# K's transposes moved from the tensor engine to a transposing DMA, with a retuned instruction order and a new ending, in a grouped-query attention kernel

## The chip, the cores and the metric

The kernel runs on one core of one Trainium2 chip. The metric is the device time of one execution in microseconds (us). Engines are named as in the profile: PE is the tensor engine (PEld its weight loads), ACT the scalar engine, DVE the vector engine, POOL GpSimd, SP the engine that only issues DMAs here. "Span" is the length of one profiled execution; the device time is about 1.8 us more.

## The reference

```python
batch, seq, n_heads, n_kv_heads, dim = 8, 512, 32, 8, 64      # float32 in and out
K_expanded = np.repeat(K, 4, axis=2); V_expanded = np.repeat(V, 4, axis=2)
scores  = np.einsum('bhqd,bhkd->bhqk', Q, K_expanded) / np.sqrt(dim)
weights = np.exp(scores - np.max(scores, axis=-1, keepdims=True))
weights = weights / (np.sum(weights, axis=-1, keepdims=True) + 1e-10)
output  = np.einsum('bhqk,bhkd->bhqd', weights, V_expanded)
```

## The kernel before

Work is cut into 32 units (8 batches, 4 pairs of KV heads). A unit has 16 score tiles of 128 x 1024. For each, PE makes two matmuls into one of three score buffers in PSUM (the pools that hold PE's results); then ACT exponentiates the tile (11 of 16), or DVE approximates the exponential with one multiply-add on the bits (5 of 16; one of these five, the "two-term" tile, gets two more operations on POOL). Between score tiles PE does "filler": blocks of weights times V (4 matmuls each), and transposes of Q and K. Filler goes through two further PSUM buffers, which DVE has to empty.

The order of all this is fixed when the program is built, by a small planner in the kernel that walks through these tables:

```python
TILES  = [int(c) for c in "0100010001020100"]   # per score tile: 0 ACT, 1 DVE, 2 DVE + POOL
SCORES = "ADAAADAADAADAADA"                     # order in which PE makes tiles for ACT and DVE
FILL   = [0, 0, 8, 0, 0, 6, 9, 0, 0, 8, 0, 0, 12, 0, 0, 9]   # filler pieces after each (sum 52)
ORDER  = "K4 o6 o7 08 o7 18 o5 o7".split()      # groups: K4 = K's 4 transposes, o6 = 6 output
SKIP   = 22                                     # blocks, 08/18 = 8 transposes of half of Q
```

SKIP is the number of filler slots left empty at the start, so it sets the phase of the groups against the fills. K arrives and is turned so:

```python
def load_k(b):
    t = kn_pool.tile([128, SC, KV * D], BF16, name="k_nat")
    nc.gpsimd.dma_start(out=t, in_=rows(K, b, 0, KV))
    kn[b] = t
...                                    # mm_turn: 4 PE transposes per unit into a filler buffer
    nc.tensor.transpose(xs[f][:, at * 128:(at + 1) * 128], src, ident)
...                                    # take_turn: one DVE copy, then two DMAs swap the halves
    nc.vector.tensor_copy(out=k[:, 0, :], in_=x[:, 0:S])
    nc.sync.dma_start(out=k[64:128, 1, :], in_=k[0:64, 0, :])
    nc.sync.dma_start(out=k[0:64, 1, :], in_=k[64:128, 0, :])
```

The softmax here doesn't subtract the row's maximum and nothing guards it: scores larger than these inputs give would overflow.

## Time and profile before

| kernel before | |
|---|---|
| device time | 352.62 us median of 4 runs (352.34 to 353.13) |
| span of the profiled run | 351.0 us |
| steady unit, from the starts of every 11th exponential | 10.34 us |
| last exponential starts | 338.8 us, 12.1 us before the end |

The first fence is from the page of the kernel before: busy time and share of the span by engine, then the chain of work that ended last, by engine and by line.

```profile
PE 336.7 (96%) x5774; PEld 224.7 (64%) x5774; DVE 331.3 (94%) x462; ACT 333.1 (95%) x355; POOL 280.2 (80%) x200
...
PE 54%; ACT 37%; DVE 3%; issue 2%; POOL 2%; DMA 1%; POOLq 0%; DVEq 0%; ACTq 0%
```

Three engines are all nearly full, and the chain alternates between two of them. A chain that alternates suggests that neither is the limit alone.

The next lines are groups of instructions of the kernel before (line, engine, operation, out<-in, shape, count | busy us, mean ns | idle before). They are the exponentials, K's transposes and the copies after them; the last two are what the change removes.

```profile
L270 ACT ACTIVATE pa<-s 128x1024 bf16<-128x1024 f32 x352 | 330.6, 1029 | 2.3 <-PE s L259 1.9
...
L382 PE MATMUL x<-ident,k_nat 128*128 128x128 bf16 x124 | 17.3, 222 | 0.0
...
L389 DVE COPY kt<-x 128x512 bf16<-128x512 bf16 x31 | 11.3, 365 | 0.0
```

The mean durations mislead here, because successive instructions overlap. What one costs an engine that is full is the step from its start to the start of the next. In the trace, exponentials follow each other at 0.903 us when nothing holds them up (not 1.029), K's transposes at 0.057 us (not 0.222) and the K copy at 0.278 us (not 0.365). ACT therefore needs 11 x 0.903 = 9.94 us per unit, and a unit takes 10.34.

The timeline of ACT shows the same (start us, length us, what, count, idle before it). One line is an unbroken run; its length over its count is the real pace, 316.10/336 = 0.941 us, which times 11 is 10.35 us.

```profile
7.90 10.19 ACT L270 ACTIVATE pa<-s 128x1024 bf16<-128x1024 f32 x11 [1.00 <-PE s L259]
18.34 316.10 ACT L270 ACTIVATE pa<-s 128x1024 bf16<-128x1024 f32 x336 [0.25 <-PE s L259]
```

Finally the end of the kernel before, from the chain of waits (start us, us, what). The last exponential is over at 339.9 us. The chain waits for POOL's two-term sum until 341.1, then for the last blocks, and then DVE divides until 346.5.

```profile
337.63 1.27 POOL hi L297
...
338.98 2.13 POOL sum L303
...
341.16 1.08 PE x L314 x29
...
343.07 2.22 issue
...
346.05 0.42 DVE o_sb L355
```

The 2.22 us called "issue" lie inside one division of 128 x 512 on DVE, which by DVE's timeline ran from 343.04 us for 2.33 us.

### The profile page before, as it was taken

How to read it: one execution, taken by the hardware profiler on the slowest of the kernel's cores; microseconds unless marked ns; L12 is line 12 of the kernel's file. 1: busy time of each engine (PE TensorE's matmuls, PEld its weight loads, DVE VectorE, ACT ScalarE, POOL GpSimd, SP SyncE). 2: the span in 40 equal slices, each digit the busy share in tenths (PEclk: the TensorE clock that was granted, in tenths of full speed). 3: DMA queues.
4: the chain of work that ended last, by engine and by line, in shares of the span. 5: the costliest groups of instructions: out<-in, count | busy, mean ns of one | idle time of the engine just before them, and what ended most of it. 6: DMA issues, size and time to landing. Idle time of an engine off the chain costs nothing.

```text
span 351.0 us, 12943 instructions
## 1 busy us (share of the span) xinstructions
PE 336.7 (96%) x5774; PEld 224.7 (64%) x5774; DVE 331.3 (94%) x462; ACT 333.1 (95%) x355; POOL 280.2 (80%) x200
## 2 busy tenths in 40 slices
PE   8799999999999999999999999999999999999981
PEld 3366666666666666666666666666666666666661
DVE  3899999999999999999999999999999999999984
ACT  3999999999999999999999999999999999999960
POOL 6368897879978797987979799787988879768783
PEclk9999999999999999999999999999999999999997
DMA  8999567997769968698787985699586997822356
GB/s 184 209 155 185 156 170 194 199 224 168 174 161 240 256 133 209 129 238 202 196 196 167 209 197 160 177 224 251 115 207 153 237 232 183 208 79 78 121 181 181
DMA packets 51479, 64.40 MB, mean 183 GB/s; under 512 B 3424, under 2 KB 36064, under 8 KB 51424
## 3 DMA queue, kind: packets, MB, share of 16 engines
q0 software_dynamic: 25344, 24.91, 47.1%
q1 hardware_dynamic: 25024, 38.28, 32.0%
q8 instruction: 45, 0.74, 0.8%
q10 hardware_dynamic: 1056, 0.39, 0.4%
q14 instruction: 10, 0.08, 0.1%
HBM read 50.86 MB, written 33.55 MB: 241 GB/s over the span
## 4 chain that ended last, share of the span: by engine, by line
PE 54%; ACT 37%; DVE 3%; issue 2%; POOL 2%; DMA 1%; POOLq 0%; DVEq 0%; ACTq 0%
ACT pa L270 37%; PE s L259 24%; PE x L314 22%; PE x L382 7%; DMA kt<-kt 1%; PE x L461 1%; DVE pd L287 1%; POOL sum L303 1%; POOL o_sb L355 1%; DVE raw L334 0%; POOL hi L297 0%; PE x L473 0%; DVE kt L474 0%; DVE inv L350 0%; DVE qt L396 0%
## 5 line engine op out<-in xcount | busy, mean ns | idle before, releaser
L270 ACT ACTIVATE pa<-s 128x1024 bf16<-128x1024 f32 x352 | 330.6, 1029 | 2.3 <-PE s L259 1.9
L259 PE MATMUL s<-qt,kt 64*128 64x512 bf16 x1024 | 163.4, 381 | 3.8 <-DVE pd L287 1.5
L287 DVE TENSOR_SCALAR pd<-s 128x1024 uint16<-128x1024 f32 x128 | 156.0, 1219 | 1.7 <-PE s L259 1.6
L314 PEld LDWEIGHTS <-pa 128*128 128x128 bf16 x2816 | 136.1, 97 | 28.9 <-issue 28.9
L314 PE MATMUL x<-v,pa 128*128 128x65 bf16 x2728 | 150.9, 194 | 0.3 <-DVE raw L334 0.3
L314 PE MATMUL x<-v,pd 128*128 128x65 bf16 x992 | 134.2, 194 | 0.0
L355 POOL TENSOR_TENSOR o_sb<-raw,inv 128x1024 f32<-128x1024 f32 x63 | 118.6, 1907 | 2.9 <-DVE inv L350 2.5
L314 PEld LDWEIGHTS <-pd 128*128 128x128 bf16 x1024 | 100.2, 98 | 0.5 <-issue 0.4
L259 PEld LDWEIGHTS <-kt 64*128 64x128 bf16 x1024 | 56.1, 93 | 68.1 <-issue 37.2
L334 DVE COPY raw<-x 128x455 f32<-128x455 f32 (+3 forms) x161 | 92.8, 578 | 6.6 <-PE x L314 5.8
L297 POOL TENSOR_TENSOR hi<-lo,shift 128x512 int32<-128x512 int32 x32 | 40.6, 1269 | 50.1 <-PE x L314 38.7
L303 POOL TENSOR_TENSOR sum<-lo,hi 128x1024 bf16<-128x1024 bf16 x32 | 68.0, 2125 | 2.5
L382 PE MATMUL x<-ident,q_nat 128*128 128x128 bf16 x504 | 43.8, 220 | 0.0
L396 DVE COPY qt<-x 128x1024 bf16<-128x1024 bf16 x63 | 42.9, 681 | 0.0
L287 DVE TENSOR_SCALAR lo<-s 128x1024 uint16<-128x1024 f32 x32 | 39.2, 1224 | 0.5 <-PE s L259 0.5
L314 PE MATMUL x<-v,sum 128*128 128x65 bf16 x248 | 34.7, 194 | 1.1 <-POOL sum L303 1.1
L382 PEld LDWEIGHTS <-q_nat 128*128 128x128 bf16 x504 | 29.9, 98 | 7.9 <-issue 7.9
L314 PEld LDWEIGHTS <-sum 128*128 128x128 bf16 x256 | 25.0, 98 | 1.2 <-POOL sum L303 1.2
L229 POOL DMA_DIRECT2D q_nat<-in_Q_dram x32 | 25.5, 797 | 0.0
L247 POOL COPY v<-v_nat 128x2048 bf16<-128x2048 bf16 x8 | 15.2, 1904 | 5.7 <-DMA v_nat<-in_V_dram 5.7
L382 PE MATMUL x<-ident,k_nat 128*128 128x128 bf16 x124 | 17.3, 222 | 0.0
L382 PEld LDWEIGHTS <-k_nat 128*128 128x128 bf16 x124 | 7.5, 98 | 7.1 <-issue 7.1
(36 smaller groups left out, 67.6 us busy)
## 6 DMA issues: line engine op xcount, KB each, us to landing
out_dram<-o_sb SPq DMA_DIRECT2D x30, 1024.0 KB, 5.2
q_nat<-in_Q_dram POOLq DMA_DIRECT2D x31, 512.0 KB, 6.0
k_nat<-in_K_dram POOLq DMA_DIRECT2D x8, 512.0 KB, 8.2
v_nat<-in_V_dram POOLq DMA_DIRECT2D x8, 512.0 KB, 10.5
kt<-kt SPq DMA_DIRECT2D x62, 64.0 KB, 5.2
out_dram<-o_sb SPq DMA_DIRECT2D x3, 512.0 KB, 3.0
q<-in_Q_dram ACTq DMA_DIRECT2D x1, 256.0 KB, 4.4
k<-in_K_dram SPq DMA_DIRECT2D x1, 256.0 KB, 3.9
```

The lines of the kernel that those rows point to most:

```text
L229: nc.gpsimd.dma_start(out=t[:, :, lo * D:], in_=rows(Q, b, HU * gp + lo, HU * (gp + 1)))
L247: nc.gpsimd.tensor_copy(out=t[:, :, :, 0:D], in_=vn.pop(b).rearrange("p sc (h d) -> p sc h d", h=KV))
L259: nc.tensor.matmul(s[:, m, :], kt[u][64 * m:64 * m + 64, 0 if m == g else 1, kc * 128:(kc + 1) * 128], qt[u][64 * m:64 * m + 64, i, :], st ...
L270: recent.append(nc.scalar.activation(out=pts[t], in_=score.pop(t), func=mybir.ActivationFunctionType.Exp, scale=float(scale),))
L287: nc.vector.tensor_scalar(out=bits, in0=score.pop(t), scalar1=float(A_schr), scalar2=float(B_two if two else B_one), op0=mybir.AluOpType.mult,
L297: nc.gpsimd.tensor_tensor(out=high.rearrange("p m s -> p (m s)").bitcast(I32), in0=bits.rearrange("p m s -> p (m s)").bitcast(I32), in1=shift,
L303: nc.gpsimd.tensor_tensor(out=dst, in0=bits.bitcast(BF16), in1=high.bitcast(BF16), op=mybir.AluOpType.add)
L314: nc.tensor.matmul(xs[f][:, at * D1:(at + 1) * D1], pts[(u * HPG + i) * SC + kc][:, m, qc * 128:(qc + 1) * 128], v1[u][:, kc, 2 * i // HPG ...
L334: nc.vector.tensor_copy(out=raws[u][:, lo:lo + n, :], in_=x[:, 0:n * D1])
L355: eng.tensor_tensor(out=osbs[u].rearrange("p qc h d -> p h qc d")[:, lo // SC + h0:lo // SC + h0 + nh], in0=src[:, :, 0:D].rearrange("p (h ...
L382: nc.tensor.transpose(xs[f][:, at * 128:(at + 1) * 128], src, ident)
L396: nc.vector.tensor_copy(out=qt[u][:, 2 * part:2 * part + 2, :], in_=x)
```

## The change

The intent: take K off PE and DVE, refit the order to the freed time, and shorten the end.

```diff
-    TILES = [int(c) for c in "0100010001020100"]
-    SCORES = "ADAAADAADAADAADA"
-    FILL = [0, 0, 8, 0, 0, 6, 9, 0, 0, 8, 0, 0, 12, 0, 0, 9]
-    ORDER = "K4 o6 o7 08 o7 18 o5 o7".split()
-    SKIP = 22
+    TILES = [int(c) for c in "0100010201000100"]
+    SCORES = "ADAADAAADAADAADA"
+    FILL = [0, 0, 7, 0, 0, 6, 0, 7, 0, 9, 0, 0, 7, 0, 0, 12]
+    ORDER = "o7 o7 08 o7 o4 18 o7".split()
+    LAST_TILES = [int(c) for c in "0000100111000100"]
+    LAST = {
+        NU - 2: ("AADADADAAADAADAA", [3, 0, 0, 3, 0, 7, 0, 0, 32, 0, 32, 0, 21, 3, 0, 18]),
+        NU - 1: ("DADADAAADAAAADAA", [0, 0, 0, 7, 0, 0, 32, 0, 0, 32, 0, 10, 10, 0, 0, 10]),
+    }
+    SKIP = 15
 # K of batches 1 to 7 (batch 0 stays on PE, units 2 and 3 now also in the start):
+        ks[b] = ks_pool.tile([S, KV * D], BF16, name="ks")          # in DRAM
+        nc.gpsimd.dma_start(out=ks[b], in_=K[b].rearrange("s h d -> s (h d)"))
+    def turn_k(b):
+        straight[b] = kt_pool.tile([128, GP, S], BF16, name="straight")
+        nc.sync.dma_start_transpose(out=straight[b], in_=ks.pop(b))
+    def swap_k(b): ...
+        nc.sync.dma_start(out=k[0:64], in_=t[64:128])
+        nc.sync.dma_start(out=k[64:128], in_=t[0:64])
 # issued one unit apart, a batch ahead:
+                if r == 4 and b + 1 < B:
+                    load_k(b + 1)
+                if r == 20 and b + 1 < B:
+                    turn_k(b + 1)
+                if r == 40 and b + 1 < B:
+                    swap_k(b + 1)
 # the ending: last exponential in two halves; the last output groups first sum over three
 # quarters of the keys ("open"), then add the last quarter ("close"); more divisions from PSUM
+        for ms in (slice(0, 1), slice(1, 2)) if t == 16 * NU - 1 else (slice(0, 2),):
+    groups += [(step, NU - 1, lo, 4) for step in ("open", "close") for lo in (3 * BLK, 3 * BLK + 4)]
 # ... planner support for the above, store and divide split for the last units: cut
```

## The prediction

> **What bounds it now.** Three engines are nearly full: PE 96%, ACT 95%, DVE 94% of 351.0 us (busy table). In the middle the kernel repeats per unit (16 score tiles: 11 exponentials on ACT, 5 on DVE). From the starts of the exponentials in the timeline, a unit takes 10.34 us. Back to back, exponentials start 0.903 us apart, so ACT needs 11 x 0.903 = 9.94 us. Summing the shortest start-to-start steps of the DVE instructions gives 9.95 us per unit. PE's steps without its waits for score buffers come to about 9.7 us (an estimate). So 0.40 us per unit is lost because three score buffers couple three engines without slack; the chain of waits alternates between PE (54%) and ACT (37%).
> The tail is loose: the last exponential starts at 338.8 us, yet the span ends at 351.0. The chain there goes DVE, POOL shift and sum (to 341.1), PE, four DVE divisions (to 346.5), store.
>
> **What changes.** (1) For batches 1 to 7, K is cast into DRAM and transposed by a DMA issued from SP; two larger DMAs swap the halves. This removes 4 PE transposes per unit (0.057 us each from start to start, 0.23 us) and one DVE copy (0.278 us start to start), 28 times. (2) Fill sizes and the place of the two-term tile are retuned. (3) The last unit has no POOL sum, splits its last exponential, sums three quarters of the last outputs before it ends, and moves the divisions.
> ACT keeps its 352 tiles (one split).
>
> **On the critical path.** Per unit, DVE falls to about 9.67 us and PE to 9.47; ACT stays at 9.94 and becomes the only limit. I expect 10.10 us per unit: about 60% of the 0.40 us lost comes back; the score buffers still make a few exponentials wait. 0.24 x 31 = 7.4 us. Tail: after the last exponential about 0.1 us extra for the split, a quarter of the last matmuls, one or two divisions of 0.5 us, then the 4.5 us that ran from the last division to the end before: 7 to 8 us instead of 12.2, so about 4.5 us. The start is unchanged.
> Sum: 352.6 - 7.4 - 4.5 = 340.7 us. I predict **340.7 us**, range **336.5 to 346.0**; faster by over 2%: 0.87; within 2%: 0.12; slower by over 2%: 0.01.
>
> **The transposing DMA.** The trace has none. The Trainium skill ("DMA: Bandwidth & Descriptors", "Latency and other measured facts") gives transposes 261 GB/s; estimated from it, 512 KB take 2 us plus a few us as the other transfers do here (K loads land in 8.2 us). The program leaves one unit (10 us) between cast and transpose, 1.25 between transpose and swap, 1.5 until use. So it should be hidden. The same page ("Anatomy of one DMA") says a semaphore wait sits on the issuing sequencer; if the transpose takes over about 20 us, SP holds up the output stores behind it.
>
> **What would show it.** PE transposes of K fall from 124 to 12, kt copies likewise from 31 to 3. Starts of the exponentials 10.0 to 10.2 us per unit. ACT leads the chain of waits, PE's share falls.  The exponentials end near 331 us and the span ends 7 to 8 us after the last one starts. No wait on the transposed K.
>
> **What would make it wrong.** The retuned order may couple worse than I assume (unit still 10.3: about 347 us) or nearly perfectly (9.96: about 336). The transposing DMA may be much slower, or crowd the Q loads (the DMA share is already 0.81 to 0.89 in the middle), delaying transposes or stores. Larger fills in the last two units may starve ACT and eat the tail's gain.

## The result, and the profile after

The changed kernel takes 345.85 us median (345.1 to 346.2, 8 runs) against 352.71 us (13 runs) for the kernel before: ratio 0.9803, 95% interval 0.9794 to 0.9813. A ratio here is the mean time of one kernel's fast runs over that of the other's of the same rounds, so not quite the ratio of the medians. That is 2.0% faster, exactly at the line between "same" and "faster", so the verdict is "unclear": certainly shorter, but not certainly by 2%. The median lies inside the predicted range by 0.15 us.

The profiled run of the changed kernel was its slowest (348.0 us, span 346.2). So I had the same kernel profiled once more, on the chip of the first batch of experiments (first experiment below): span 344.4 us, time 346.2. Both profiles are used.

From the page of the changed kernel, the same two parts:

```profile
PE 332.6 (96%) x5662; PEld 220.9 (64%) x5662; DVE 317.6 (92%) x435; ACT 330.3 (95%) x356; POOL 274.7 (79%) x199
...
ACT 62%; PE 24%; issue 4%; DVE 4%; POOL 3%; DMA 1%; SPq 0%; DVEq 0%; POOLq 0%
```

The chain now leads through ACT (62%, and 71% in the second profile). The removed groups are gone but for batch 0, as these groups show:

```profile
L423 PE MATMUL x<-ident,k_nat 128*128 128x128 bf16 x12 | 1.5, 223 | 0.0
L430 DVE COPY kt<-x 128x512 bf16<-128x512 bf16 x3 | 1.3, 419 | 0.8 <-PE x L423 0.8
```

The timeline of ACT in the second profile of the changed kernel: the long run has a pace of 300.12/323 = 0.929 us, 10.22 us per unit. But the start is broken into pieces, and so is the end from 320 us on, which in the kernel before was one run until 334.

```profile
7.90 4.74 ACT L306 ACTIVATE pa<-s 128x1024 bf16<-128x1024 f32 x5 [0.94 <-PE s L293]
12.79 1.02 ACT L306 ACTIVATE pa<-s 128x1024 bf16<-128x1024 f32 x1 [0.15 <-PE s L293]
14.17 4.81 ACT L306 ACTIVATE pa<-s 128x1024 bf16<-128x1024 f32 x5 [0.36 <-PE s L293]
19.43 300.12 ACT L306 ACTIVATE pa<-s 128x1024 bf16<-128x1024 f32 x323 [0.45 <-PE s L293]
320.00 2.85 ACT L306 ACTIVATE pa<-s 128x1024 bf16<-128x1024 f32 x3 [0.44 <-PE s L293]
323.55 1.94 ACT L306 ACTIVATE pa<-s 128x1024 bf16<-128x1024 f32 x2 [0.70 <-PE s L293]
```

The end, from the timeline of DVE (second profile). There is no POOL sum and no long division in it; DVE is done 2.6 us after the last tile's first half began (338.53 us), where in the kernel before it took 7.6 us from the last tile's start (338.83 to 346.47).

```profile
338.72 0.42 DVE L396 TENSOR_TENSOR o_sb<-x,inv 128x256 f32<-128x256 f32 x1
339.98 0.18 DVE L391 RECIPROCAL inv<-x 128x4 f32<-128x4 f32 x1 [0.83 <-PE x L352]
340.20 0.42 DVE L396 TENSOR_TENSOR o_sb<-x,inv 128x256 f32<-128x256 f32 x1
340.54 0.17 DVE L391 RECIPROCAL inv<-x 128x4 f32<-128x4 f32 x1
340.75 0.42 DVE L396 TENSOR_TENSOR o_sb<-x,inv 128x256 f32<-128x256 f32 x1
```

Cutting each profiled span at the starts of the exponentials tells where the time went. The two columns in the middle are experiments that follow. All figures are us.

| stretch | before | ending only | middle only | changed (second profile) |
|---|---|---|---|---|
| to the first exponential | 7.90 | 7.38 | 7.90 | 7.90 |
| units 0 to 3 | 41.45 | 41.67 | 41.99 | 42.36 |
| units 4 to 29 (26 units) | 269.02 | 269.00 | 265.53 | 265.52 |
| unit 30 | 10.45 | 13.74 | 10.20 | 12.54 |
| unit 31, to its last tile | 10.01 | 11.21 | 9.73 | 10.21 |
| from there to the end | 12.13 | 5.89 | 12.66 | 5.91 |
| span | 351.0 | 348.9 | 348.0 | 344.4 |

So the middle gives 3.5 us (0.134 us in each of 26 units), the ending gives 6.2 us after the last tile's start but costs 2.3 us in units 30 and 31, and the start costs 0.9 us. The exponentials as a whole are over no earlier than before: the last tile starts at 338.5 against 338.8 us.

In the first profile the start cost more: units 0 to 3 took 44.70 us. PE stood still twice with nothing to wait for that the profile shows, and unit 3 took 12.28 us in place of 10.22. (Another 0.7 us lies in unit 1, where PE waited 0.6 us for POOL's two-term sum.) The experiments come back to the pauses.

### The profile page after: what moved, and what is told of

Same layout as the page of the kernel before. It is cut to its first block, busy times and chain, and to the rows that moved or that the text cites. A ratio compares the mean times of both kernels' runs of the same rounds, so it can differ in the third digit from the quotient of the medians.

```text
span 346.2 us, 12636 instructions
## 1 busy us (share of the span) xinstructions
PE 332.6 (96%) x5662; PEld 220.9 (64%) x5662; DVE 317.6 (92%) x435; ACT 330.3 (95%) x356; POOL 274.7 (79%) x199
## 4 chain that ended last, share of the span: by engine, by line
ACT 62%; PE 24%; issue 4%; DVE 4%; POOL 3%; DMA 1%; SPq 0%; DVEq 0%; POOLq 0%
ACT pa L306 62%; PE x L352 11%; PE s L293 11%; PE x L423 3%; DVE pd L323 2%; DMA v<-in_V_dram 1%; DVE raw L375 1%; POOL sum L339 1%; POOL v L281 1%; POOL q_nat L248 0%; POOL hi L333 0%; DVE inv L391 0%; DVE qt L437 0%; DVE lo L323 0%; DVE o_sb L396 0%
## 5 line engine op out<-in xcount | busy, mean ns | idle before, releaser
L396 POOL TENSOR_TENSOR o_sb<-raw,inv 128x1024 f32<-128x1024 f32 (+1 forms) x64 | 118.5, 1867 | 50.9 <-DVE inv L391 50.9
L293 PE MATMUL s<-qt,straight 64*128 64x512 bf16 x448 | 142.8, 382 | 1.0
L293 PE MATMUL s<-qt,swapped 64*128 64x512 bf16 x448 | 141.8, 381 | 0.3 <-ACT pa L306 0.3
L375 DVE COPY raw<-x 128x455 f32<-128x455 f32 (+1 forms) x159 | 87.9, 570 | 14.2 <-PE x L352 14.2
L339 POOL TENSOR_TENSOR sum<-lo,hi 128x1024 bf16<-128x1024 bf16 x31 | 65.9, 2126 | 2.4
L293 PEld LDWEIGHTS <-straight 64*128 64x128 bf16 x448 | 36.1, 93 | 31.6 <-issue 21.4
L293 PEld LDWEIGHTS <-swapped 64*128 64x128 bf16 x448 | 33.0, 93 | 21.3 <-issue 13.9
L323 DVE TENSOR_SCALAR lo<-s 128x1024 uint16<-128x1024 f32 x31 | 37.7, 1215 | 0.0
L293 PE MATMUL s<-qt,kt 64*128 64x512 bf16 x128 | 21.3, 381 | 2.9 <-ACT pa L306 0.9
```

Source lines behind the costliest of these rows:

```text
L293: nc.tensor.matmul(s[:, m, :], kt[u][int(m != g)][64 * m:64 * m + 64, kc * 128:(kc + 1) * 128], qt[u][64 * m:64 * m + 64, i, :], start=Tru ...
L323: nc.vector.tensor_scalar(out=bits, in0=score.pop(t), scalar1=float(A_schr), scalar2=float(B_two if two else B_one), op0=mybir.AluOpType.mult,
L339: nc.gpsimd.tensor_tensor(out=dst, in0=bits.bitcast(BF16), in1=high.bitcast(BF16), op=mybir.AluOpType.add)
L375: nc.vector.tensor_copy(out=raws[u][:, lo:lo + n, :], in_=x[:, 0:n * D1])
L396: eng.tensor_tensor(out=osbs[u].rearrange("p qc h d -> p h qc d")[:, lo // SC + h0:lo // SC + h0 + nh], in0=src[:, :, 0:D].rearrange("p (h ...
```

## The experiments

Theory A: nearly all of the gain is the ending, plus a smaller gain in the middle than predicted; the rest of the middle's gain never came. Rival B: the middle gave the 7.4 us of the prediction, and something else took it back.

### The changed kernel again, each half alone, and no K transfers

The first needs no edit. For the second and third, the middle's tables and K's path, or the last units' tables and the ending, were put back as in the kernel before:

```diff
 # ending only                               # middle only
-    TILES/SCORES/FILL/ORDER/SKIP: new       -    LAST_TILES, LAST: new
+    TILES/SCORES/FILL/ORDER/SKIP: old       +    LAST_TILES = TILES; LAST = {}
-    K by transposing DMA                    -    split exponential, open/close, new divisions
+    K by PE, as before                      +    ending as before
```

The fourth gives a wrong result: batches 1 to 7 use batch 0's K.

```diff
-        ks[b] = ...; nc.gpsimd.dma_start(out=ks[b], ...)    # and the transpose, and the swaps
+            kt[GP * b + gp] = kt[gp]
```

Expected of the changed kernel again:

> The changed kernel once more, for a second profile. If the two pauses of PE inside a block (1.2 and 0.7 us, at 42 and 51 us, at instructions 961 and 1217 of PE, 256 apart) are late instruction pages, they need not come back; the time without profile should be 345.9 us as before. Units in the middle 10.2 us each.

Expected of the ending alone:

> The kernel before with only the last two units' schedule and the new ending. Theory A (nearly all of the gain is the ending; the shorter units are eaten by a slower start): about 4 us off, 348.5 us. Rival B (as predicted: units give 7.4 and the tail 4.5, but something else gives back 5): also 348. It is the middle-only run that tells them apart: A and B differ there.

Expected of the middle alone:

> The changed kernel with the old last unit and the old ending: K by transposing DMA and the retuned cycle only. Theory A: units of 10.21 in place of 10.34 us give 27 x 0.13 = 3.5 us, the slower start takes 1 to 3.4 us back: 349.5 to 352 us. Rival B (the prediction's step): 7.4 us off, 345 us.

Expected without K transfers:

> Wrong on purpose: batches 1 to 7 use K of batch 0, so casting, transposing and swapping DMAs are gone and all compute instructions stay. If the K transfers cost time by crowding other transfers (Q, instruction pages) in the start, 1 to 3 us faster than the changed kernel, with no PE pause at 42 and 51 us and units 2 and 3 at 10.2 us. If they are hidden, the same time within 0.5 us.

| run | median us (range), runs | ratio, 95% |
|---|---|---|
| changed kernel again | 346.17 (345.91 to 347.31), 4 | 0.9818 (0.9798 to 0.9837) |
| ending only | 350.78 (350.3 to 350.92), 4 | 0.9940 (0.9925 to 0.9954) |
| middle only | 350.75 (349.79 to 353.88), 4 | 0.9971 (0.9921 to 1.0021) |
| no K transfers (wrong) | 345.84 (345.37 to 346.1), 4 | 0.9801 (0.9786 to 0.9815) |

The kernel before was at 352.84 us beside them; the two later batches ran on other chips, with the kernel before at 352.54 and 352.81 us. In the second profile of the changed kernel the pauses of PE at 42 and 51 us did not come back. Middle only is nowhere near B's 345 us, and its units are 10.21 us, so B falls. A's figure for the ending alone (348.5) was missed too: it gives 2 us, not 4, because unit 30 grows to 13.74 us there and unit 31 to 11.21, against 12.54 and 10.21 beside the new middle. So "nearly all of the gain is the ending" does not hold either: in the changed kernel the middle gives 3.5 us and the ending 3.9 net. Together the halves give 6.6 us of span; one by one they give 2.1 and 3.0 (the profile of middle only is its fastest run). Why units 30 and 31 are shorter beside the new middle was not tested; I suppose that less output work is pending when the ending begins. The tables of the ending were also chosen for the new middle, and in the kernels with other middles (this one and the two refits below) these two units take 23.1 to 25.9 us together, against 22.7.

Without any K transfer the time is that of the changed kernel. So in a typical run the K transfers are hidden, and they are not what keeps a unit at 10.21 us. Unit 0 took 11.91 us even so: the slower start is not the transfers either. Its spread is small (345.4 to 346.1), which matters below.

### Is it the freed time or the new order?

One run takes K off PE but keeps the old cycle; the other keeps K on PE and takes the new cycle.

```diff
 # K by DMA, old cycle
-    TILES = "0100010201000100"; SCORES = "ADAADAAADAADAADA"; SKIP = 15
-    FILL = [0, 0, 7, 0, 0, 6, 0, 7, 0, 9, 0, 0, 7, 0, 0, 12]; ORDER = "o7 o7 08 o7 o4 18 o7"
+    TILES = "0100010001020100"; SCORES = "ADAAADAADAADAADA"; SKIP = 15
+    FILL = [0, 0, 6, 0, 0, 4, 9, 0, 0, 8, 0, 0, 12, 0, 0, 9]; ORDER = "o6 o7 08 o7 18 o5 o7"
 # K on PE, new cycle (against the ending-only kernel)
-    SKIP = 22; FILL and ORDER old
+    SKIP = 15; FILL = [0, 0, 9, 0, 0, 6, 0, 9, 0, 9, 0, 0, 7, 0, 0, 12]
+    ORDER = "K4 o7 o7 08 o7 o4 18 o7"; TILES and SCORES new
```

> The changed kernel with the old cycle of the middle (old place of the two-term tile, old order of scores, old groups of outputs; two fills smaller by 2 because K's 4 transposes are gone). If the freed PE and DVE time makes the units shorter: about 10.2 us in the middle, as with the new cycle. If the retuned order does it: 10.3 us, as before.

> K transposed on PE as before, with the new cycle (two fills larger by 2 to hold K's transposes) and the new ending. If the freed time makes the units shorter: 10.3 us or more in the middle. If the retuned order does it: 10.2 us.

Both failed as tests, and instructively. They took 365.81 us (ratio 1.0367) and 404.37 us (1.1458), with units of 10.86 and 12.13 us. Neither outcome had been foreseen. A third run of the same batch failed in the same way:

```diff
 # unit 0 alone in the old cycle; all later units as in the changed kernel
+    FIRST_TILES = "0100010001020100"
     LAST = {
+        0: ("ADAAADAADAADAADA", [0, 0, 8, 0, 0, 6, 9, 0, 0, 8, 0, 0, 12, 0, 0, 9]),
```

> The changed kernel, but unit 0 alone in the old cycle. If the slower start is the new order's (the fifth score tile goes to DVE one place earlier, ACT runs dry twice): unit 0 back from 11.5 to 10.4 us and about 1 us off in all, 345 us. If it is the K transfers or the extra K transposes of the start: unit 0 stays above 11 us.

It took 387.68 us (1.0994). Unit 0 was 10.59 us as hoped, but each later unit was 11.59 us, although their tables had not been touched. From its waits (who waited for whom, us in total, times, longest us):

```profile
ACT pa L308 <- PE s L295: 43.1, 68, 1.3
DVE pd L325 <- PE s L295: 24.1, 62, 1.2
...
PE x L354 <- DVE qt L439: 17.1, 59, 0.4
```

PE waits 59 times, about twice per unit, for a filler buffer that DVE has not emptied, and ACT then waits for PE. The cause is a sum: unit 0's fills came to 52, all later ones to 48, so the output groups were displaced by 4 pieces against the fills for the rest of the run. Groups that used to end with a fill now straddled two fills, and the next group needed the buffer at once. The fourth run of the batch had the same fault, so it says nothing on its own question:

```diff
-        NU - 2: ("AADADADAAADAADAA", [3, 0, 0, 3, 0, 7, 0, 0, 32, 0, 32, 0, 21, 3, 0, 18]),
+        NU - 2: ("AADADADAAADAADAA", [6, 0, 0, 8, 0, 8, 0, 0, 12, 0, 12, 0, 12, 6, 0, 12]),
```

> As the one before, and in the second last unit the output work is spread evenly (6 to 12 blocks per gap in place of 32, 32 and 21). If ACT starves there because of the large fills: that unit falls from 12.5 to 11 us or less, and about 1 us comes off. If that work had to be done anyway: the time moves into the last unit and the total stays within 0.5 us.

It took 388.02 us (1.0998), the same as its sibling within 0.4 us; its unit 30 was 12.53 against 12.47 us. Whether the large fills of unit 30 cost anything stays open.

### The same questions, with the fills in step

```diff
 # K by DMA, old cycle, in step
-    FILL = [0, 0, 6, 0, 0, 4, 9, 0, 0, 8, 0, 0, 12, 0, 0, 9]; SKIP = 15
+    FILL = [0, 0, 6, 0, 0, 6, 9, 0, 0, 8, 0, 0, 12, 0, 0, 7]; SKIP = 12
 # K on PE, new TILES, SCORES and FILL refitted
-    SCORES = "ADAAADAADAADAADA"; ORDER = "K4 o6 o7 08 o7 18 o5 o7"; SKIP = 22
-    FILL = [0, 0, 8, 0, 0, 6, 9, 0, 0, 8, 0, 0, 12, 0, 0, 9]
+    SCORES = "ADAADAAADAADAADA"; ORDER = "K4 o7 o7 o4 08 18 o7 o7"; SKIP = 24
+    FILL = [0, 0, 10, 0, 0, 7, 0, 5, 0, 10, 2, 0, 9, 0, 0, 9]
 # unit 0 in the old order, its fills summing to 48
-        0: ("ADAAADAADAADAADA", [0, 0, 8, 0, 0, 6, 9, 0, 0, 8, 0, 0, 12, 0, 0, 9]),
+        0: ("ADAAADAADAADAADA", [0, 0, 7, 0, 0, 6, 9, 0, 0, 8, 0, 0, 9, 0, 0, 9]),
```

> The old cycle without K's transposes again, now with the fills in step: the two fills that held K each lose 2, and the filler starts so that the first output group of a unit begins with a fill. The run before it was out of step by 3 blocks and took 10.86 us per unit. If the freed PE and DVE time alone makes the units short: 10.2 us. If the retuned order is needed: 10.25 to 10.35 us.

> K on PE with the new places of the DVE tiles, and fills, groups and start chosen anew so that they are in step (the best of some 150,000 tried with the kernel's own planner, which gives this one 10.41 us per unit where it gives the changed kernel 10.12 and the kernel before 10.28). If the retune alone made the units short, it would reach 10.2 us on the chip; if K has to leave PE first, 10.35 us or more.

> Unit 0 alone in the old order of scores, with fills that sum to 48, so that the later units stay in step (in the run before they summed to 52, and every later unit took 11.59 us). If the out-of-step fills were the whole of that loss: 10.21 us per unit again. If the slower start is the new order's: unit 0 at 10.4 to 10.6 us in place of 11.1 to 11.9, and 0.5 to 1 us off: 345 us.

| K | cycle | steady unit, us | time, us (median, or each fast run) |
|---|---|---|---|
| on PE | old (kernel before) | 10.34 | 352.8 |
| on PE | new, refitted | 10.41 | 353.15 |
| by DMA | old, in step | 10.28 (profile slow) | 350.35 and 353.42 (the two fast runs; ratio 0.9976) |
| by DMA | new (changed kernel) | 10.21 | 346.2 |

All with the new ending, but the first. From the first row to the second a unit loses 0.07 us, from the first to the third it gains 0.06, and both together gain 0.13. So neither part does it alone: the freed time is needed, and without the retuned order half of the gain is lost. The third row is weaker evidence than the others. Its profiled run is slow: two units of 15.0 us, with the pauses described next, lie in it. The 10.28 is the median of units 4 to 29, and the granted clock is 1.00 in the undisturbed stretch from 130 to 270 us. Without the excess of the two long units (9.8 us) its span of 358.2 us would be 348.4; the span of its fastest run was 348.6, which fits the same unit. The refit of the second row is the best that I found with the kernel's own planner, not a proof that there is no better one.

The last of the three settles the displaced fills: with 48 in place of 52, and nothing else changed, later units are 10.21 us again, not 11.59. It also shortens the start: units 0 to 2 take 31.28 us against 32.15 in the second profile of the changed kernel. Yet its median is 348.08 us (345.21 to 348.94, 6 runs; ratio 0.9853), slower than the changed kernel. Its unit 3 took 14.56 us. The timeline of PE in it:

```profile
40.79 0.25 PE L354 MATMUL x<-v,pa 128*128 128x65 bf16 x3
43.88 0.19 PE L354 MATMUL x<-v,pd 128*128 128x65 bf16 x1 [2.83 <-issue]
43.91 0.25 PE L354 MATMUL x<-v,pa 128*128 128x65 bf16 x3
```

And the first profile of the changed kernel at its own pause:

```profile
42.10 0.25 PE L352 MATMUL x<-v,pa 128*128 128x65 bf16 x3
43.54 0.19 PE L352 MATMUL x<-v,pd 128*128 128x65 bf16 x1 [1.19 <-issue]
```

PE stops in the middle of one output block, before a matmul that has no semaphore to wait for. Counting PE's instructions (matmuls and weight loads) from the start, the pause falls before number 961 in both, and before 961 again in the run without most Q transposes below; the second pause of the changed kernel's first profile (50.52 to 51.38 us) is at 1217, which is 256 more. The Trainium skill ("Runtime: NRT & Kernel Launch", "Instruction fetch mechanics") says that instructions are fetched in blocks of 16 KiB, 256 instructions, by a DMA queue of the sequencer's own, and calls the cost of crossing a block "mostly hidden". The trace agrees with the blocks: the queue of kind "instruction" moved one packet of 16,384 bytes about every 7.4 us. In the paused runs the packet was late. In the changed kernel's first profile it ran from 41.25 to 42.20 us and PE went on at 43.54; in the run with unit 0 in the old order from 41.52 to 42.46, after PE had already stopped at 40.85, and PE went on at 43.88. In the fast profiles of all kernels here, 573 packets in all, a packet starts at most 182 PE instructions after PE entered the block before it; the only five exceptions (195 to 255) are these two, the one before the second pause (209), and two in the run without most Q transposes. The two pauses of the run in the slow state (3.5 and 3.4 us from start to start) fall before numbers 3521 and 9153, again multiples of 256 from 961, each with a packet that started only after PE had stopped.

Why were they late? The first transposing DMA was in flight then. From the timelines of SP, first the run with unit 0 in the old order, then the second profile of the changed kernel, which had no such pause:

```profile
24.97 8.44 SPq L265 DMA_TRANSPOSE straight<-ks  x1
43.61 0.47 SPq L270 DMA_DIRECT2D swapped<-straight  x1
```

```profile
24.45 6.18 SPq L263 DMA_TRANSPOSE straight<-ks  x1
36.73 0.47 SPq L268 DMA_DIRECT2D swapped<-straight  x1
```

SP issues the swap as soon as the transpose has landed, so these lines give its duration: 18.6 us in the paused run (landed 43.6), 12.3 us in the other; 16.7 us in the changed kernel's first profile. The three fast profiles with such a pause have first transposes of 16.7, 18.5 and 18.6 us; the five others with K by DMA have 12.3 to 15.5 us and no pause, and none of the five without a transposing DMA has one. That the instruction packets queue behind the transpose is my reading; the runs show that the two come together, not the queueing itself. Crowded DMA engines that delay both would look the same, and no run separates the two. It fits that the kernels without a transposing DMA keep the ranges of their timed runs within 1.4 us (ending only: 350.3 to 350.9), while among those with it some reach 4 us (middle only: 349.8 to 353.9).

### What still lies between 10.21 us and ACT's 9.94

From unit 4 on the units share unit 3's Q, 7 of 8 transposes are left out and the copies cut to an eighth, in an otherwise unchanged order. Its output is wrong, which doesn't matter for the time.

```diff
+        if u >= 4 and at:
+            return
         nc.tensor.transpose(xs[f][:, at * 128:(at + 1) * 128], src, ident)
...
-            nc.vector.tensor_copy(out=qt[u][:, 2 * part:2 * part + 2, :], in_=x)
+            if u >= 4:
+                qt[u] = qt[3]
+                nc.vector.tensor_copy(out=junk, in_=x[:, 0:128])
```

> Wrong on purpose: from unit 4 on Q is unit 3's, 1 of 8 transposes of each Q group is left and a copy of 128 columns in place of 1024; the order of all instructions is the changed kernel's. It takes some 0.8 us of PE and 0.9 us of DVE out of each unit. If the 0.27 us that a unit still lies above ACT's 9.94 us come from PE and DVE being nearly full: 9.95 to 10.0 us per unit. If they come from the score buffers and the fixed order (fills of 7 blocks that ACT's two waiting tiles just cover): 10.1 to 10.2 us.

346.62 us median (345.27 to 348.23, 4 runs; 0.9828). Busy times in the stretch from 103.4 to 206.8 us (stretch, its length, then busy us and count of PE, PEld, DVE, ACT and POOL; clock; DMA share; GB/s), for the kernel before, the changed kernel's second profile and this run:

```profile
103.40:206.80 103.40, 103.12 (x1802) 69.64 (x1800) 101.83 (x141) 103.29 (x111) 87.25 (x62) 1.00 0.89 198
```

```profile
103.40:206.80 103.40, 103.12 (x1788) 69.56 (x1788) 99.08 (x132) 103.37 (x112) 87.67 (x61) 1.00 0.95 209
```

```profile
103.40:206.80 103.40, 100.27 (x1652) 60.19 (x1651) 91.11 (x133) 103.40 (x113) 87.39 (x62) 1.00 0.95 214
```

DVE has 8 us less to do in ten units, PE's weight loads 9 us less, and yet a unit is still 10.17 us, 0.04 less than in the changed kernel. So the remaining 0.23 us are not a lack of PE or DVE time. The profiled execution, the slowest of the four, lost time in its start instead: units 0 to 3 took 44.87 us, with the pause before 961 and then a wait for K itself. Its first transpose took 18.5 us, the swapped K of batch 1 landed at 52.39 us, and PE had to wait for it (from the waits between 50 and 53 us):

```profile
PE s L293 <- DMA swapped<-straight: 1.4, 1, 1.4
```

This is the only profile in which the score matmuls waited for K from the transposing DMA.

In the trace of a steady unit of the changed kernel, two or three exponentials per unit start 0.02 to 0.15 us late, most of them about 0.04 us after the end of their score matmul, and that matmul follows a fill which PE began only after ACT had released a score buffer. The order of work around the three score buffers sets the pace. I take that as the cause, but it is argued from the trace: no run gave the kernel a fourth buffer.

## Why the prediction was right or wrong

The time of 345.85 us lies in the range of 336.5 to 346.0, but that is partly luck: 0.15 us more would have missed it, and the same kernel measured again gave 346.17. Of the 11.9 us foreseen (352.6 to 340.7), 6.9 came. The middle, the ending and the start each fell short, so these errors added up; only inside the ending did two of them partly cancel.

- *"I expect 10.10 us per unit: about 60% of the 0.40 us lost comes back"*: this is the step that was mis-sized. It measured 10.21 us; a third (0.134 of 0.40 us) came back, 3.5 us in place of 7.4. The mechanism was right in part: freed PE and DVE time did shorten the unit, by 0.06 us without a new order (the weaker row of the table) and 0.13 with it, and ACT came to lead the chain. What was over-estimated is how much slack on PE and DVE returns. The run with light Q transposes freed more of both and gained only 0.04 us, so what is left is not slack; that it is the order around the three score buffers is argued from the trace, not shown.
- *"Tail ... about 4.5 us"*: the net is 3.9 us, by a different sum. From the last tile's start to the end it took 5.9 us, better than the 7 to 8 expected; but units 30 and 31 grew by 2.3 us. The prediction had named that risk (larger fills in the last two units). Its marker "the exponentials end near 331 us" was wrong by more than 7 us.
- *"The start is unchanged"*: wrong. Units 0 to 3 took 0.9 us more, and 3.3 us more in the profile with the pauses. The order of scores in unit 0 is part of it: the old order there shortened units 0 to 2 by 0.9 us.
- *"So it should be hidden"*: right for K itself in the changed kernel, since the kernel without K transfers takes the same time. The margin was thin, though: in the run with light Q transposes PE waited 1.4 us for K. A transpose took 8.4 us in the median and 16.7 us once in the first profile, not the 2 us plus a few that were estimated from the skill's 261 GB/s. The wait for it did sit on SP, as the prediction cites: in that profile SP had issued the first transpose by 32.1 us and issued nothing more until it landed at 41.4. The prediction had no place for PE's instruction stream, which paused beside the slow transposes.
- *"PE transposes of K fall from 124 to 12, kt copies likewise from 31 to 3. ... ACT leads the chain of waits"*: right.

No experiment with a correct result beats the changed kernel in median. The nearest, unit 0 in the old order, has one run of 345.21 us, no better than the changed kernel's best (345.1); whether that run was free of pauses is not known, since only the slowest was profiled.

## What to carry to other kernels

When several engines run in lockstep over few buffers, freed engine time is worth little by itself: here it needed a new order, and a displacement of the groups by 4 pieces cost 1.4 us per unit, ten times what the change won per unit. So when a piece of work leaves a fixed schedule, check first that groups and fills still end together. And cut the two traces at the same landmarks, from start to end: the total fell just inside the predicted range although the start, the middle and the end each did something else than foreseen.

## What the Trainium skill lacked or had wrong

- "Runtime: NRT & Kernel Launch", "Instruction fetch mechanics": crossing a 16 KiB block is called mostly hidden. In runs with a slow transposing DMA it was not: PE stood 0.9 to 3.0 us from start to start in fast profiles, at numbers 961 and 1217, which are 256 instructions apart. The same section gives PE 2048 instructions of memory, and also says that the next page is fetched while the current one runs. The trace fits the second: PE stopped at the end of a block when the packet for the next one was late (it had started 209 to 255 instructions into that block).
- No page has what follows the packet: PE went on 1.3 to 1.4 us after the packet's end (42.20 to 43.54, 42.46 to 43.88 us).
- "DMA: Bandwidth & Descriptors", "Latency and other measured facts": 261 GB/s for a transposing DMA (with a non-contiguous middle dimension). Here 512 KB of bf16 from DRAM beside other transfers took 7.4 to 16.7 us from issue to landing in the first profile (median 8.4, which is 62 GB/s), and 4.5 to 18.6 us over all runs. The page has no figure for a transpose beside other transfers.
- No page gives a time for which the issue of a transpose of this size keeps SP on Trainium2: 1.3 to 10.3 us in these runs, against 0.4 to 0.7 us for most plain copies.
